# Block stages of a gated MLP: chains 256 columns wide, and weight tiles moved by 64 bytes against the activations

## The chip, the cores and the metric

The kernel runs on one core of one Trainium2 chip. Its time is the device time of one execution in microseconds (us); times of a kernel are given as the median of several runs, and one more execution is taken by the hardware profiler. A core has a matrix engine (TensorE; PE in the profile, with its weight loads shown apart as PEld), a vector engine (VectorE, DVE), a scalar engine (ScalarE, ACT), GpSimd (POOL) and SyncE (SP), which here issues most of the transfers from device memory (DMAs). They work side by side and wait for each other through semaphores. A matmul multiplies a stationary operand of 128 x 128 values, which is loaded first, with a moving operand of 128 rows and up to 512 columns, and writes or adds into a bank of PSUM. Everything else lies in SBUF, 128 partitions wide; the place of a tile is its byte address within each partition.

## The reference

Two layers over 512 rows of width 1024. Layer A mixes by a gated matrix memory and by attention to a memory of 256 rows, layer B by attention over a band of chunks and by the same kind of memory attention. Behind each mixer stands a gated MLP with a causal convolution of width 3, and this is the part that the change is about:

```python
def conv_ffn(h, w_up, conv_w, conv_b, w_down):
    u, g = jnp.split(h @ w_up, 2, axis=-1)
    g = causal_dwconv(g, conv_w, conv_b)
    return (jax.nn.silu(g) * u) @ w_down
...
        x = x + jnp.concatenate([mix_out, mem_out], axis=-1) @ w_out
        x = x + conv_ffn(rmsnorm(x, norm_ffn_g[l]), ffn_w_up[l], ffn_conv_w[l], ffn_conv_b[l], ffn_w_down[l])
```

The inner width D_FF is 2816, that is 22 tiles of 128. All data are float32.

## The kernel before

**High and low parts.** A product of float32 matrices is made of three matmuls in a faster format (fp32r): high part times high part, high times low, low times high. `split` makes the two parts: ScalarE copies the source into the high tile (line 130), VectorE subtracts it from the source into the low tile (line 131). `mm3` issues the three matmuls (lines 177, 178, 179); the order of their stationary operands is high, high, low. `load` fetches raw weights into a tile "wr" (line 143, issued by SP), and `parts` splits them into tiles "wh" and "wl", of which there are three each.

**Channel mixer.** For every tile j of the inner width the mixer computes an up and a gate product, applies the convolution and the activation, and keeps the result in `hid`. For j = 0 to 4 (`plain`) these are ordinary projections: 8 blocks of weights, 24 matmuls of 512 columns each. From j = 5 (PLAIN) to 21, 17 steps a layer, `later` and `step` use a block scheme with seven products of half size in place of eight. The rows are taken in two halves of H = 256 columns. `forms` prepares sums and differences of the activations once a layer, in "u" tiles: a tile of `self.sums` holds the high part in its first 256 columns and the low part in the others. Class `Forms` prepares the weights of a step: the upper block (`split_up`: a11, a12) and the sums (`split_sums`: s1, s3) go to wh and wl; three further forms, s2, a22 and s4, are made by `form` in two "u" tiles each.

**A step.** `step` writes out the order by hand for TensorE, ScalarE and VectorE (`manual_schedule`). Its chains on TensorE are a11, a12, s2, a down product, s1, s3, a second down product, a22, s4. Between them stand the preparation of the next step's weights (`nxt`) and the tail of the last one (`tail`: convolution, activation, gating, split). A down product is 12 matmuls of 512 columns with weights of `ffn_w_down`; steps 9 to 20 have two, steps 5 to 8 one, step 21 none. `products` is a chain over four blocks, with mm3 on 256 columns: 12 matmuls. For j in WIDE (9 to 20) the chains s2, s3 and a22 are made by `wide_products` instead: per block one matmul of the low weights with 256 columns, and one of the high weights with 512, the activations' high and low parts side by side (lines 792 and 793). The two halves of the bank are then added up: a copy by ScalarE (line 827) and an addition by VectorE (line 829).

**Places.** Tiles of one tag lie one after another in the order in which tags are first used. "u", "pt", "wr" and "t" all begin at 64 modulo 512 bytes, and so do the activations. wh and wl have rows of D + 64 values (4352 bytes, 256 more than a multiple of 512), so their three buffers begin at 64, 320 and 64 (wh) and 320, 64 and 320 (wl). `parts` takes `at=SHIFT`, 16 values or 64 bytes further, for the two splits of the block stages.

**Around the stages.** Everything outside the step loop is ordered by a planner that simulates the engines. x is kept in eight "u" tiles (`xT`), written to device memory (`xspill`), dropped, and read again by `reload_x` (line 423, on SP) behind each channel mixer and ahead of each output projection. The down products of a step are added into `xspill` by a transfer of POOL (line 761). The last six tiles of `hid` go through an ordinary projection after the loop, whose result is added to xT (line 1281 in layer A). The B layer's values are "u" tiles too (`project_pair`).

Of the kernel before, what the change touches and what calls it, by code (L numbers as in the profile page):

```python
# [9 lines left out]
F32 = mybir.dt.float32  # L10
# [6 lines left out]
P = 128  # L17
# [26 lines left out]
UNITS = {PLAIN - 1: (0, 1, 2, 3), 5: (None, 4), 6: (None, 5), 7: (None, 6), 8: (None, 7)}  # L44
UNITS.update((j, (2 * j - 10, 2 * j - 9)) for j in range(9, 21))

WIDE = range(9, 21)
H = S // 2


# [5 lines left out]
def trunk(  # L56
# [22 lines left out]
    pool = ctx.enter_context(tc.tile_pool(name="pool", bufs=1))  # L79
    psum = ctx.enter_context(tc.tile_pool(name="psum", bufs=1, space=bass.MemoryType.PSUM))  # L80

    bufs = {"wr": 3, "wh": 3, "wl": 3, "u": 57, "t": 8, "pt": 2, "s": 16, "rb": 3, "bias": 4}
    pbufs = {"mm": 3, "sc": 3, "tr": 2}
    count = [0]
    dram = ctx.enter_context(tc.tile_pool(name="dram", bufs=1, space=bass.MemoryType.DRAM))
# [1 line left out]
    def sb(tag, shape, dtype=F32):  # L87
        count[0] += 1
        return pool.tile(shape, dtype, tag=tag, name=f"{tag}{count[0]}", bufs=bufs[tag])
# [2 lines left out]
        count[0] += 1  # L92
        return psum.tile([P, S], F32, tag=tag, name=f"p{tag}{count[0]}", bufs=pbufs[tag])

    def small(n=4):
        return sb("s", [P, 32])[:, :n]


    ident = cpool.tile([P, P], F32, name="ident")
# [45 lines left out]
            nc.sync.dma_start(raw[:, :, b:], extra)  # L145
        return raw

    SHIFT = 16

    def weight_tiles(a, b, at=0):  # L150
        places = (at, at)
        return [
            sb(tag, [P, D + 64], F32R)[:, o : o + a * b].rearrange("p (a b) -> p a b", a=a)
            for tag, o in zip(("wh", "wl"), places)
        ]

    def parts(raw, pinned=False, at=0):
        _, a, b = raw.shape
        hi, lo = weight_tiles(a, b, at)
        split(hi, lo, raw, pinned=pinned)  # L160
        return hi, lo

# [68 lines left out]

    def diagonal(c):

        cs = [sb("s", [P, 32], F32R)[:, :TT] for _ in range(2)]
        split(*cs, c, on_act=False)
        dgs = []
        for c in cs:
            dg = sb("t", [P, S], F32R)
            V.tensor_tensor(
                out=dg.rearrange("p (a b) -> p a b", a=TT),  # L240
                in0=ident.unsqueeze(1).to_broadcast([P, TT, P]),
                in1=f(c).unsqueeze(2).to_broadcast([P, TT, P]),
                op=ALU.mult,
            )
            dgs.append(dg)
        return dgs
# [150 lines left out]
    def x_tile(j):  # L397
        tp = ps(("sc", "tr")[j % 2])
        for T in range(TT):
            nc.tensor.transpose(tp[:, T * P : (T + 1) * P], xr[T][:, j * P : (j + 1) * P], ident)  # L400
        xT.append(sb("u", [P, S]))
        A.copy(xT[j], tp)

    acts, scaled_x = [], []
# [14 lines left out]

    def reload_x():  # L420
        for j in range(KT):
            xT[j] = sb("u", [P, S])
            tc.keep_in_program_order(nc.sync.dma_start(xT[j], xspill[j]))

    def value_weights(hf, u):
# [222 lines left out]
    class ChannelMixer:  # L648
# [136 lines left out]

            return [(p[i - 1][:, :H], p[i - 1][:, H:]) for p in self.sums]

        def wide_products(self, r, w, i):

            n = KT // 2  # L790
            for k, p in enumerate(self.sums):
                nc.tensor.matmul(r[:, :H], w[1][:, k], p[i - 1][:, :H], start=False, stop=False, skip_group_check=True)  # L792
                nc.tensor.matmul(r, w[0][:, k], p[i - 1], start=False, stop=k == n - 1, skip_group_check=True)  # L793

        def later(self):


            prep, tail = Forms(self, PLAIN), None
            prep.sums()
            prep.split_second()  # L800
            prep.sum_third()
            prep.split_up()
            prep.split_sums()
            prep.sum_fourth()
            prep.split_down()
            prep.split_gate()
            with tc.manual_schedule(
                engines={mybir.EngineType.PE, mybir.EngineType.Activation, mybir.EngineType.DVE}
            ):
                for j in range(PLAIN, FT):  # L810
                    self.beside()
                    tail, prep = self.step(j, prep, Forms(self, j + 1) if j + 1 < FT else None, tail)
            for part in (tail.last_block, tail.first_tap, tail.second_tap, tail.third_tap, tail.gated, tail.split):
                part()

        def step(self, j, w, nxt, tail):
            def then(o, *names):
                for name in names if o is not None else ():
                    getattr(o, name)()

            def sum_products(o, r, w, i):

                if j in WIDE:
                    self.wide_products(r, w, i)
                else:
                    self.products(r, w, self.t(i))
                A.copy(o, r[:, :H])  # L827
                if j in WIDE:
                    V.tensor_tensor(out=o, in0=o, in1=r[:, H:], op=ALU.add)  # L829

            new = Tail(self, j)
            then(tail, "last_block", "first_tap")
            w.split_fourth()
            r1, r2, new.r3 = ps("mm"), ps("mm"), ps("sc")
            new.up, new.u3, new.pre = sb("t", [P, S]), sb("t", [P, S]), sb("t", [P, S])
            self.products(r1, w.a11, self.b(0, 0), True)
            A.copy(new.up[:, :H], r1[:, :H])
            then(tail, "second_tap")
            self.products(r2, w.a12, self.b(1, 0), True)
            V.tensor_tensor(out=new.up[:, :H], in0=new.up[:, :H], in1=r2[:, :H], op=ALU.add)  # L840
            then(tail, "third_tap")
            sum_products(new.up[:, H:], r1, w.s2, 2)
            then(nxt, "sums")
            then(tail, "gated")
            then(nxt, "split_second", "sum_third")
            w.down_products(0)
            self.products(new.r3, w.s1, self.t(1), True)
            w.add_down(0)
            then(tail, "split")
            then(nxt, "split_up")  # L850
            sum_products(new.u3[:, :H], r1, w.s3, 3)
            V.tensor_tensor(out=new.pre[:, H:], in0=new.u3[:, :H], in1=new.r3[:, :H], op=ALU.add)
            then(nxt, "split_sums")
            w.down_products(1)
            then(nxt, "sum_fourth")
            w.add_down(1)
            sum_products(new.pre[:, :H], r1, w.a22, 4)
            then(nxt, "split_down", "split_gate")
            self.products(new.r3, w.s4, self.b(1, 1))
            return new, nxt  # L860

    class Forms:
# [12 lines left out]
            return t[:, :n], t[:, n:]  # L875

        def form(self, src):
            hi, lo = (sb("u", [P, S], F32R).rearrange("p (a b) -> p a b", a=KT // 2) for _ in range(2))
            split(hi, lo, src)
            return hi, lo  # L880

# [13 lines left out]
            self.sub(self.halves(self.s13)[1], self.halves(self.up)[0], self.halves(self.gate)[0])  # L895

        def split_up(self):
            self.a11, self.a12 = zip(*(self.halves(t) for t in parts(self.up, at=SHIFT)))

        def split_sums(self):  # L900
            self.s1, self.s3 = zip(*(self.halves(t) for t in parts(self.s13, at=SHIFT)))

        def sum_fourth(self):
            s2, s4 = self.halves(self.s24)
# [48 lines left out]
    def channel_mixer(l, act, norm, gain, beside):  # L953

        mixer = ChannelMixer(l, act, norm, gain, beside)
        forms = mixer.forms()
        run(mixer.plain(0))
        for j in range(1, UNSCALED):
            weave(mixer.plain(j), forms, KT / (16.0 * (UNSCALED - 1)))
        until(lambda: len(mixer.ready) == KT, forms)  # L960
        mixer.buffers()
        for j in range(UNSCALED, PLAIN):
            units = UNITS.get(j, ())
            raws = {u // 2: mixer.load_down(u // 2) for u in units[::2]}
            weave(mixer.plain(j), forms, 4 / (16.0 * (PLAIN - UNSCALED)))
            for u in units:
                if u // 2 not in mixer.down:
                    mixer.down[u // 2] = parts(raws[u // 2])
                mixer.add(*mixer.down_products(u))
        run(forms)  # L970
        mixer.later()
        reload_x()
        return mixer.hid[FT - LAST :]
# [328 lines left out]
    def project_pair(j):  # L1302
        def times_row(o):
            t = sb("t", [P, S])
            V.tensor_tensor(out=t, in0=o, in1=norm.row, op=ALU.mult)
            return t

        ov = yield from project(w_kv, AW + j * P, kvact)
        t = times_row(ov) if norm.row is not None else None
        o = yield from project(w_kv, j * P, kvact)  # L1310
        if t is None:
            t = times_row(ov)
        k = head_keys(times_row(o))
        tp = ps("mm")
        for T in range(TT):
            nc.tensor.transpose(tp[:, T * P : (T + 1) * P], t[:, T * P : (T + 1) * P], ident)
        v = []
        for i in range(2):

            w = sb("u", [P, S], F32R).rearrange("p (h c) -> p h c", h=4)  # L1320
            split(w[:, :, :HD], w[:, :, HD:], tp[:, i * MEM : (i + 1) * MEM].rearrange("p (h c) -> p h c", h=4))
            v += [w[:, :2, :], w[:, 2:, :]]
        q = queries((yield from project(b_w_in, j * P, act)), norm.row)
        qkv[j] = q, k, v
# [206 lines left out]
```

## Time and profile before

| | us |
|---|---|
| three runs: median, lowest, highest | 1191.7, 1190.5, 1192.39 |
| the profiled execution | 1191.35 |
| its span, first to last instruction | 1189.6 |
| TensorE busy | 1179.0 |
| VectorE busy | 961.9 |
| ScalarE busy | 723.6 |

In rows of instruction groups, the columns are: line, engine, operation, tiles written and read (out<-in, without buffer numbers), shapes, count, then busy time in us, mean duration of one in ns, and the idle time ahead of them with what ended it. Matmuls are pipelined: the duration of one reaches from its start to the last result, and the next one starts long before that. The pace is the distance between two starts, so it is read from the timeline, whose columns are start and duration in us, engine, line, operation, tiles, count.

### The profile page before, as it was taken

To read this page: it belongs to the slowest core of one execution; us is meant where nothing else is said; L and a number is where in the kernel's file an instruction comes from. 1 tells how busy PE (TensorE), PEld (TensorE's weight loads), DVE (VectorE), ACT (ScalarE), POOL (GpSimd) and SP (SyncE) were. 2 spreads that over 40 slices of the span, in tenths; PEclk is the share of its full clock that TensorE was granted. 3 is DMA by queue.
4 is the path that set the end of the run, shared out by engine and by line. 5 is a ranking of instruction groups with operands and counts; after the bars stand their busy time and mean duration, and the time that the engine had idled before them with its cause. 6 is when DMAs were issued, how large, how long until landed. Compare 5 with 4: busy or idle time off the path is not lost.

```text
span 1189.6 us, 18184 instructions
## 1 busy us (share of the span) xinstructions
PE 1179.0 (99%) x6719; PEld 1032.1 (87%) x6719; DVE 961.9 (81%) x1760; ACT 723.6 (61%) x1294; POOL 130.0 (11%) x222
## 2 busy tenths in 40 slices
PE   9999999999999999999999999999999999999997
PEld 8988888888889988999888888888889988999986
DVE  6877688888978888888798888997896888888855
ACT  5648677655655555555576667776565655555545
POOL 1211201010021111111021000101001010111100
PEclk9999999999999999999999999999999999999999
DMA  8645313444266666666564313245326466665551
GB/s 283 212 114 133 93 55 80 146 142 135 87 160 159 158 162 158 154 145 132 145 197 131 89 53 102 70 131 184 117 89 152 107 141 142 142 141 137 123 159 71
DMA packets 200155, 158.61 MB, mean 133 GB/s; under 512 B 8344, under 2 KB 179838, under 8 KB 200066
## 3 DMA queue, kind: packets, MB, share of 16 engines
q1 hardware_dynamic: 183906, 119.74, 34.3%
q0 software_dynamic: 15584, 36.67, 15.3%
q8 instruction: 53, 0.87, 0.3%
q10 hardware_dynamic: 576, 1.05, 0.2%
q14 instruction: 36, 0.29, 0.1%
HBM read 128.89 MB, written 32.46 MB: 136 GB/s over the span
## 4 chain that ended last, share of the span: by engine, by line
PE 92%; ACT 3%; DVE 2%; DMA 2%; issue 0%; SPq 0%; POOL 0%; POOLq 0%; DVEq 0%; ACTq 0%
PE pmm L177 15%; PE pmm L178 15%; PE pmm L179 14%; PE ptr L178 6%; PE ptr L177 6%; PE ptr L179 6%; PE pmm L793 6%; PE psc L179 5%; PE psc L178 5%; PE psc L177 5%; PE pmm L792 3%; PE psc L527 2%; DMA wr<-in_mem_w_kv_dram 2%; PE ptr L1358 1%; PE ptr L1379 1%; PE ptr L1380 1%
## 5 line engine op out<-in xcount | busy, mean ns | idle before, releaser
L177 PE MATMUL pmm<-u,wh 128*128 128x512 f32 (+1 forms) x872 | 307.6, 353 | 0.3 <-ACT u L130 0.2
L179 PE MATMUL pmm<-u,wl 128*128 128x512 f32 (+1 forms) x872 | 304.7, 350 | 0.0
L178 PE MATMUL pmm<-u,wh 128*128 128x512 f32 (+1 forms) x872 | 304.6, 350 | 0.0
L131 DVE TENSOR_TENSOR wl<-wr,wh 128x1024 fp32r<-128x1024 f32 (+3 forms) x172 | 199.8, 1162 | 56.8 <-ACT wh L130 54.9
L130 ACT CAST wh<-wr 128x1024 fp32r<-128x1024 f32 (+3 forms) x172 | 171.8, 1001 | 98.4 <-PE pmm L178 44.3
L179 PEld LDWEIGHTS pmm<-u,wl 128*128 128x128 f32 x872 | 163.9, 188 | 21.0
L177 PEld LDWEIGHTS pmm<-u,wh 128*128 128x128 f32 x872 | 164.3, 189 | 18.5 <-ACT u L130 1.1
L178 PEld LDWEIGHTS pmm<-u,wh 128*128 128x128 f32 x872 | 164.2, 188 | 18.2 <-DVE u L131 0.5
L177 PE MATMUL ptr<-u,wh 128*128 128x512 f32 x272 | 106.7, 392 | 0.0
L178 PE MATMUL ptr<-u,wh 128*128 128x512 f32 x272 | 106.2, 390 | 0.0
L179 PE MATMUL ptr<-u,wl 128*128 128x512 f32 x272 | 106.0, 390 | 0.0
L761 POOL DMA_DIRECT2D xspill<-t x64 | 55.5, 867 | 454.2 <-ACT t L760 443.5
L130 ACT CAST u<-pt 128x512 fp32r<-128x512 f32 x102 | 62.7, 617 | 46.9 <-DVE pt L883 46.8
L131 DVE TENSOR_TENSOR u<-pt,u 128x512 fp32r<-128x512 f32 x102 | 69.9, 688 | 11.0 <-ACT u L130 8.3
L177 PE MATMUL psc<-u,wh 128*128 128x256 f32 (+1 forms) x232 | 75.9, 327 | 0.0
L179 PE MATMUL psc<-u,wl 128*128 128x256 f32 (+1 forms) x232 | 75.7, 326 | 0.0
L178 PE MATMUL psc<-u,wh 128*128 128x256 f32 (+1 forms) x232 | 75.6, 326 | 0.0
L793 PE MATMUL pmm<-u,u 128*128 128x512 f32 x192 | 69.9, 398 | 0.0
L945 ACT ACTIVATE t<-t 128x512 f32<-128x512 f32 x34 | 21.5, 633 | 79.4 <-DVE t L668 79.4
L829 DVE TENSOR_TENSOR t<-t,pmm 128x256 f32<-128x256 f32 x72 | 30.1, 419 | 41.8 <-ACT t L827 41.8
L760 ACT COPY t<-ptr 128x512 f32<-128x512 f32 x64 | 37.4, 585 | 42.9 <-PE ptr L179 42.8
L668 DVE SCALAR_TENSOR_TENSOR t<-t,cols,t 128x511 f32<-128x511 f32 x80 | 59.7, 746 | 3.7 <-ACT t L675 3.7
(300 smaller groups left out, 2670.6 us busy)
## 6 DMA issues: line engine op xcount, KB each, us to landing
wr<-in_ffn_w_up_dram SPq DMA_DIRECT2D x54, 512.0 KB, 4.2
wr<-in_ffn_w_down_dram SPq DMA_DIRECT2D x38, 512.0 KB, 4.1
pt<-in_ffn_w_up_dram SPq DMA_DIRECT2D x34, 512.0 KB, 6.4
xspill<-t POOLq DMA_DIRECT2D x64, 256.0 KB, 5.3
wr<-in_a_w_in_dram SPq DMA_DIRECT2D x20, 512.0 KB, 3.8
xspill<-u POOLq DMA_DIRECT2D x32, 256.0 KB, 2.7
u<-xspill SPq DMA_DIRECT2D x32, 256.0 KB, 4.8
wr<-in_w_kv_dram SPq DMA_DIRECT2D x12, 512.0 KB, 3.8
```

The lines of the kernel that those rows point to most:

```text
L130: high = A.copy(hi, src) if on_act else V.tensor_copy(hi, src)
L131: low = V.tensor_tensor(out=lo, in0=src, in1=f(hi), op=ALU.subtract)
L177: nc.tensor.matmul(o, lh, rh, start=first, stop=False, skip_group_check=more)
L178: nc.tensor.matmul(o, lh, rl, start=False, stop=False, skip_group_check=more)
L179: nc.tensor.matmul(o, ll, rh, start=False, stop=last, skip_group_check=more)
L527: nc.tensor.matmul(o, a, b, start=first and i == 0, stop=i == 1)
L668: V.scalar_tensor_tensor(acc[:, n:], src[:, : S - n], self.fw[:, c * FT + j : c * FT + j + 1], acc[:, n:], op0=ALU.mult, op1=ALU.add,)
L760: A.copy(t, o)
L761: G.dma_start(xspill[j], t, accum_op=ALU.add)
L792: nc.tensor.matmul(r[:, :H], w[1][:, k], p[i - 1][:, :H], start=False, stop=False, skip_group_check=True)
L793: nc.tensor.matmul(r, w[0][:, k], p[i - 1], start=False, stop=k == n - 1, skip_group_check=True)
L829: V.tensor_tensor(out=o, in0=o, in1=r[:, H:], op=ALU.add)
```

## The change

- `wide_products` and WIDE go; all chains of all 17 steps are made by `products`, 256 columns wide, and the additions at line 829 go with them.
- The order of tags in memory is fixed at the start by allocating one tile of each. Sizes are chosen so that the places modulo 512 come out as wanted: wh and wl become single tiles wh0, wh1, wh2 and wl0, wl1, wl2, of which the first two pairs have 16 values to spare.
- Ordinary weights take these in a ring, high and low parts both at the activations' place (64). Block weights take fixed ones, the upper block 0 and the sums 1; their high parts lie at 0, their low parts at 128 modulo 512, 64 bytes below and above the activations.
- The forms s2, a22 and s4 leave "u" for new tags "fh" (high, at 0) and "fl" (low, at 128), four buffers each. xT takes the same eight tiles, and so do the B layer's values except those of pair 5. "u" has 50 buffers in place of 57.
- Small tiles become 16 values wide instead of 32, 26 in place of 16, spread over three tags that also fill gaps between the others.
- In `later` the first step's `split_up` comes first. In the plain part the ring is moved on so that it stands right when the block stages begin.

```diff
-WIDE = range(9, 21)
...
-    bufs = {"wr": 3, "wh": 3, "wl": 3, "u": 57, "t": 8, "pt": 2, "s": 16, "rb": 3, "bias": 4}
+    HALF = 16
+    sizes = {"u": (50, S), "pt": (2, 5 * S), "wr": (3, D), "t": (8, S), "wh2": (1, D), "wl2": (1, D), "rb": (3, S)}
+    sizes.update({"bias": (4, S), "wl0": (1, D + HALF), "fl": (4, S), "s0": (6, 16), "wh0": (1, D + HALF)})
+    sizes.update({"wl1": (1, D + HALF), "s1": (6, 16), "fh": (4, S), "wh1": (1, D + HALF), "s2": (14, 16)})
+    bufs = {tag: n for tag, (n, _) in sizes.items()}
...
+    for tag, (n, size) in sizes.items():
+        pool.tile([P, size], F32, tag=tag, name=f"first_{tag}", bufs=n)
...
-    SHIFT = 16
-
-    def weight_tiles(a, b, at=0):
-        places = (at, at)
-        return [
-            sb(tag, [P, D + 64], F32R)[:, o : o + a * b].rearrange("p (a b) -> p a b", a=a)
-            for tag, o in zip(("wh", "wl"), places)
-        ]
+    turn = [0]
+
+    def weight_tiles(a, b, block=None):
+        i = turn[0] % 3 if block is None else block
+        turn[0] = i + 1
+        tiles = []
+        for tag in ("wh", "wl"):
+            t = sb(f"{tag}{i}", [P, D + HALF * (i < 2)], F32R)
+            at = HALF if i < 2 and (block is None) == (tag == "wh") else 0
+            tiles.append(t[:, at : at + a * b].rearrange("p (a b) -> p a b", a=a))
+        return tiles
...
-        xT.append(sb("u", [P, S]))
+        xT.append(sb("fh" if j < KT // 2 else "fl", [P, S]))
...
-            xT[j] = sb("u", [P, S])
+            xT[j] = sb("fh" if j < KT // 2 else "fl", [P, S])
...
-        def wide_products(self, r, w, i):
-            n = KT // 2
-            for k, p in enumerate(self.sums):
-                nc.tensor.matmul(r[:, :H], w[1][:, k], p[i - 1][:, :H], start=False, stop=False, skip_group_check=True)
-                nc.tensor.matmul(r, w[0][:, k], p[i - 1], start=False, stop=k == n - 1, skip_group_check=True)
...
+            prep.split_up()
             prep.sums()
             prep.split_second()
             prep.sum_third()
-            prep.split_up()
...
-                if j in WIDE:
-                    self.wide_products(r, w, i)
-                else:
-                    self.products(r, w, self.t(i))
+                self.products(r, w, self.t(i))
                 A.copy(o, r[:, :H])
-                if j in WIDE:
-                    V.tensor_tensor(out=o, in0=o, in1=r[:, H:], op=ALU.add)
...
-            hi, lo = (sb("u", [P, S], F32R).rearrange("p (a b) -> p a b", a=KT // 2) for _ in range(2))
+            hi, lo = (sb(tag, [P, S], F32R).rearrange("p (a b) -> p a b", a=KT // 2) for tag in ("fh", "fl"))
...
-            self.a11, self.a12 = zip(*(self.halves(t) for t in parts(self.up, at=SHIFT)))
+            self.a11, self.a12 = zip(*(self.halves(t) for t in parts(self.up, block=0)))
...
-            self.s1, self.s3 = zip(*(self.halves(t) for t in parts(self.s13, at=SHIFT)))
+            self.s1, self.s3 = zip(*(self.halves(t) for t in parts(self.s13, block=1)))
...
+        skips = -(turn[0] + 1) % 3
         for j in range(1, UNSCALED):
+            turn[0] += j <= skips
             weave(mixer.plain(j), forms, KT / (16.0 * (UNSCALED - 1)))
...
-            w = sb("u", [P, S], F32R).rearrange("p (h c) -> p h c", h=4)
+            w = sb("u" if j == 5 else ("fh", "fl")[i], [P, S], F32R).rearrange("p (h c) -> p h c", h=4)
```

More of the change, by code (lines that the diff above doesn't have):

```diff
@@ L93, in ps, with small @@
         return psum.tile([P, S], F32, tag=tag, name=f"p{tag}{count[0]}", bufs=pbufs[tag])
-    def small(n=4):
-        return sb("s", [P, 32])[:, :n]
+    for tag, (n, size) in sizes.items():
+        pool.tile([P, size], F32, tag=tag, name=f"first_{tag}", bufs=n)
+    smalls = [0]
+    def small(n=4, dtype=F32):
+        smalls[0] += 1
+        i = smalls[0] % 26
+        return sb("s0" if i < 6 else "s1" if i < 12 else "s2", [P, 16], dtype)[:, :n]
     ident = cpool.tile([P, P], F32, name="ident")
@@ L146, in load, with parts @@
         return raw
-    SHIFT = 16
-    def weight_tiles(a, b, at=0):
-        places = (at, at)
-        return [
-            sb(tag, [P, D + 64], F32R)[:, o : o + a * b].rearrange("p (a b) -> p a b", a=a)
-            for tag, o in zip(("wh", "wl"), places)
-        ]
-    def parts(raw, pinned=False, at=0):
+    turn = [0]
[8 more added lines that the diff above has]
+        return tiles
+    def parts(raw, pinned=False, block=None):
         _, a, b = raw.shape
-        hi, lo = weight_tiles(a, b, at)
+        hi, lo = weight_tiles(a, b, block)
         split(hi, lo, raw, pinned=pinned)
@@ L232, in diagonal @@
     def diagonal(c):
-        cs = [sb("s", [P, 32], F32R)[:, :TT] for _ in range(2)]
+        cs = [small(TT, F32R) for _ in range(2)]
         split(*cs, c, on_act=False)
```

## The prediction

> **What bounds the kernel now.** I read the page first: busy time by engine, then the chain that ended last.
>
> ```profile
> span 1189.6 us, 18184 instructions
> PE 1179.0 (99%) x6719; PEld 1032.1 (87%) x6719; DVE 961.9 (81%) x1760; ACT 723.6 (61%) x1294; POOL 130.0 (11%) x222
> PE 92%; ACT 3%; DVE 2%; DMA 2%; issue 0%; SPq 0%; POOL 0%; POOLq 0%; DVEq 0%; ACTq 0%
> ```
>
> TensorE is busy for 99% of the span and holds 92% of the chain that ended last. What the change is worth must therefore be read from the pace at which matmuls follow one another, and not from a wait. The mean duration of a group does not tell that pace, because matmuls overlap. I read the timeline of TensorE for two steps of the block stages: one that uses the 512-wide form (a wide step) and one that does not (a plain step). I noted where the first matmul of each chain starts, and asked for the weight loads in the stretches between these starts. Columns: stretch, its length, busy time and count of the loads, granted clock, DMA share, GB/s.
>
> ```profile
> 438.72:440.09 1.37, 1.37 (x13) 1.00 0.90 236
> 440.09:441.45 1.36, 1.36 (x13) 1.00 1.16 255
> 441.45:442.87 1.42, 1.24 (x10) 1.00 0.94 253
> 442.87:445.61 2.74, 2.25 (x13) 1.00 1.06 302
> 445.61:447.02 1.41, 1.41 (x12) 1.00 0.70 176
> 447.02:448.43 1.41, 1.23 (x9) 1.00 0.02 5
> 448.43:451.17 2.74, 2.25 (x12) 1.00 0.84 101
> 451.17:452.58 1.41, 1.22 (x8) 1.00 0.01 1
> 452.58:454.02 1.44, 1.44 (x13) 1.00 0.35 20
> ```
>
> These nine stretches are the nine chains of a wide step in the order of the code: a11, a12, s2 (wide), a down product, s1, s3 (wide), a down product, a22 (wide), s4. The counts take in neighbours that overlap a border; by the code a 256-wide chain has 12 matmuls, a wide one 4 of 256 and 4 of 512 columns, a down product 12 of 512. In the 256-wide chains loads are in progress all the time, in the others not. The plain step:
>
> ```profile
> 341.87:343.29 1.42, 1.42 (x13) 1.00 1.11 228
> 343.29:344.70 1.41, 1.41 (x13) 1.00 0.81 147
> 344.70:346.14 1.44, 1.44 (x13) 1.00 0.99 51
> 346.14:347.55 1.41, 1.41 (x13) 1.00 0.86 176
> 347.55:348.97 1.42, 1.42 (x14) 1.00 1.08 352
> 348.97:351.71 2.74, 2.25 (x13) 1.00 0.27 109
> 351.71:353.14 1.43, 1.42 (x12) 1.00 0.05 12
> 353.14:354.58 1.44, 1.44 (x13) 1.00 0.55 146
> ```
>
> Here: a11, a12, s2, s1, s3, one down product, a22, s4. Twelve matmuls of one shape at a granted clock of 1.00 take 1.36, 1.41 or 1.44 us: 113, 118 or 120 ns each. The code tells which is which. Chains whose weights lie in the "u" tiles, at the activations' own place modulo 512 bytes, take 1.43 or 1.44 (s2, a22, s4 of the plain step; s4 of the wide one). Chains in wh and wl, which SHIFT = 16 moves by 64 bytes, take 1.41 or 1.42, and in the wide step a11 and a12 take 1.36. By the tile sizes, a11 and a12 have their highs 64 and their lows 320 bytes past the activations' place in both steps, and s1 and s3 in these two steps have 320 and 64. So a shift is worth 2 ns a matmul always and 6 ns sometimes, and one place is seen at two paces. The two paces in rows, the end of a12 and the end of s4:
>
> ```profile
> 441.00 0.28 PE L179 MATMUL pmm<-u,wl 128*128 128x256 f32 x1
> 441.11 0.28 PE L177 MATMUL pmm<-u,wh 128*128 128x256 f32 x1
> 441.23 0.28 PE L178 MATMUL pmm<-u,wh 128*128 128x256 f32 x1
> 441.34 0.28 PE L179 MATMUL pmm<-u,wl 128*128 128x256 f32 x1
> ...
> 453.66 0.28 PE L177 MATMUL psc<-u,u 128*128 128x256 f32 x1
> 453.78 0.28 PE L178 MATMUL psc<-u,u 128*128 128x256 f32 x1
> 453.90 0.28 PE L179 MATMUL psc<-u,u 128*128 128x256 f32 x1
> ```
>
> Starts are 0.11 to 0.12 apart in the first group (0.34 over three) and 0.12 in the second. A floor can be read too. The down products stream 512 columns and their loads leave slack (2.25 of 2.74 busy); 2.74 / 12 is 228 ns, or 114 for 256 columns. So 113 ns is about what the stream of 256 columns needs by itself, and 118 and 120 are that plus something the weight loads add. I do not expect any place to go much below 1.36 a chain.
>
> **The change part by part.** The base is the profiled execution: 1191.35 us, 1.75 above its span and 0.35 under the median of the runs. The code has 17 steps in each of two layers: j = 9 to 20 are wide, 12 a layer, the other 5 plain. Its row confirms the count (192 and 96 matmuls at line 792, 12 in a wide step, make 24):
>
> ```profile
> L792 PE MATMUL pmm<-u,u 128*128 128x256 f32 x192 | 53.9, 281 | 0.0
> L792 PE MATMUL pmm<-u,wl 128*128 128x256 f32 x96 | 27.0, 281 | 0.0
> L829 DVE TENSOR_TENSOR t<-t,pmm 128x256 f32<-128x256 f32 x72 | 30.1, 419 | 41.8 <-ACT t L827 41.8
> ```
>
> Wide chains become 256 wide. A wide step's seven block chains add up to 1.37 + 1.36 + 1.42 + 1.41 + 1.41 + 1.41 + 1.44 = 9.82 us, a plain step's to 1.42 + 1.41 + 1.44 + 1.41 + 1.42 + 1.43 + 1.44 = 9.97. Afterwards every step has seven chains of twelve 256-wide matmuls, all with highs 64 bytes below and lows 64 above the activations' place. If c is the length of one such chain, the change is 24 x (7c - 9.82) + 10 x (7c - 9.97) = 238c - 335.4 us. It is nothing at c = 1.409, so a pace of 117.4 ns decides the sign.
>
> What c will be no row shows, for no stationary tile of these chains lies 64 bytes below its activations. The bounds are the rows nearest to it: 1.36 (highs at 64, lows at 320, its best) gives 238 x 1.36 - 335.4 = -11.7 us; 1.44 (no shift) gives +7.3. A price below 1.36 I exclude to within some hundredths by the 114 ns of the down products. Both of the new places are 64 bytes away, as in the rows at 1.36 and at 1.41. I take the lower row plus an entry cost. That 1.36 is reached by a shifted pair and held for a whole chain shows that loads can run without delaying the next matmul; what keeps other chains at 1.41 seems to be how they are entered. The wide step's a11 pays 0.01 on its way down to it. I allow 0.04 a step for entries behind other kinds of chain, two down products and the step's start: 34 x 0.04 = 1.4 us. Sum: -11.7 + 1.4 = -10.3 us.
>
> The additions behind the wide chains go: 72 of 0.419 us on VectorE. They are off the path:
>
> ```profile
> 438.72:454.02 15.30, 15.30 (x99) 13.77 (x98) 12.76 (x20) 8.71 (x17) 2.93 (x4) 1.00 0.71 158
> ```
>
> VectorE is busy 12.76 of the 15.30 us of a wide step and TensorE all of it. I price the additions at nothing. If a step shrinks to 15.0, VectorE needs 12.76 - 3 x 0.42 = 11.5 of it, so it does not become the bound.
>
> Ordinary weights move too: highs and lows, until now 256 bytes apart, both come to the activations' place. That touches the 512-wide chains, all plain projections among them. Their loads have 0.49 us of slack in 2.74; the dearest place seen adds 0.08 to twelve loads (1.44 against 1.36) and disappears in it. Zero; without that slack it would be the 0.08 a chain.
>
> Buffers: "u" goes from 57 to 50, and eight tiles "fh" and "fl" carry x, the forms and most of the B layer's values. In a step s2, a22 and s4 are three pairs on four buffers; a form of the next step takes the buffer of a chain that ended before the copy which stands ahead of its split on ScalarE, so no wait is added. The reload of x behind a layer's last step now needs the buffers of that step's forms:
>
> ```profile
> 585.81 3.81 SPq L423 DMA_DIRECT2D u<-xspill  x8
> 587.52 0.28 PE L179 MATMUL psc<-u,u 128*128 128x256 f32 x1
> 594.67 2.67 SPq L143 DMA_DIRECT2D wr<-in_ffn_w_down_dram  x2
> u<-xspill SPq DMA_DIRECT2D x32, 256.0 KB, 4.8
> L1281 DVE TENSOR_TENSOR u<-u,pmm x8: 680/686/689, 594.6 to 619.8; 128x512 f32<-128x512 f32 x8
> ```
>
> The loads are issued from 585.81 and s4 ends about 587.6. The last buffer pair is free then, its load lands at 587.6 + 4.8 = 592.4, and the eight additions that read x run from 594.6 to 619.8, one about every 3.6 us, so x is there in time. What is queued behind these loads on SP is the last two weight loads of those down products, issued at 594.67, so a hold until 587.6 is covered. Without that cover it would be up to those 2 us a layer. Splitting the upper block first, and skipping weight slots in the plain part so that the ring arrives at slot 0, can make single weight splits wait. TensorE hardly waits for splits now:
>
> ```profile
> L177 PE MATMUL pmm<-u,wh 128*128 128x512 f32 (+1 forms) x872 | 307.6, 353 | 0.3 <-ACT u L130 0.2
> ```
>
> 0.3 us of idle time in 872 matmuls. I take zero for buffers and slots together, with 3 us (2 for a reload, the rest for splits) as the dear end and -1 as the cheap one, since the order outside the block stages is newly planned.
>
> Sum: 1191.35 - 10.3 = 1181.05, and with the 0.35 to the median 1181.4; I write 1181.5.
>
> A rule speaks against the core of this. The Trainium skill, page "SBUF — State Buffer", section "Who interferes with whom", gives TensorE two independent read ports, one for the moving operand and one for weight loads, and says that it never waits on anyone. By this rule the place of a weight could not matter and the change would gain nothing, where the rows above give one shape of chain three lengths by its place. The measurement decides for the sum; what would follow if the lengths came from something else than place is the fourth rival.
>
> **The rivals.** First, a part of the chains settles at 1.36 and the rest at 1.41: a place that needs the right entry, as a11 and a12 do, which take 1.42 and 1.41 in the plain step. With half of them c is 1.385: 238 x 1.385 - 335.4 = -5.8, 1186 us. A buffer wait of 3 us on top of the forecast gives much the same.
>
> Second, all chains stay at 1.41 to 1.42, like most shifted rows: c = 1.415 gives +1.4, 1193.1 us. For it: s1, s3 and the plain step's a11 are shifted by 64 and do not get lower, and the low a11 comes right behind an unshifted s4 of a wide step, whose disturbed pace (it follows a wide chain) vanishes with the change. Against it: nothing says that 64 below behaves like 320 past.
>
> Third, the slower side: highs 64 bytes below collide like highs at the same place, so all chains take 1.44. The place is the load of the next weight beside the stream of the current matmul, the price 7 ns a matmul over the floor, and it decides from c = 1.409 on. Here the wide form, whose loads have slack (1.24 of 1.42), was the cover, and it is gone. 238 x 1.44 - 335.4 = +7.3, 1199 us. For it: 1.44 is the length of all chains in "u" that are not wide, and a place before the moving data may be read just behind or just ahead of it. Against it: every chain with 64 bytes between the two places is shorter.
>
> Fourth, the place does nothing and each chain keeps the pace that its neighbours and its position give it. Then the wide s2, s3 and a22 become 1.44, 1.41 and 1.43 as in the plain step, which costs 0.02 + 0 + 0.02 a step, 24 x 0.04 = 1.0, so 1192.7 us. Against it: in the plain step the lengths alternate with the tile that the weights lie in, and not with the neighbours.
>
> **How the numbers follow.** The forecast has 0.45 (its own range 1177 to 1186: entries and buffers from -1 to +3 with a chain between 1.345 and 1.375), the first rival 0.17, the second 0.13, the third 0.15, the fourth 0.05; 0.05 is left for waits above 3 us. What this kernel's measurement can tell from no change is 0.2%, 2.4 us. Faster by more: forecast and first rival, 0.62 less the few cases near the border, 0.60. Within: the fourth and most of the second, 0.15. Slower: the third, the rest of the second and the long waits, 0.25. The range goes from 1177 to 1196: it takes in the forecast, the first, second and fourth and the mild cases of the third; its dear end and what lies below 1.34 a chain are left out.
>
> **What would show it.** In the changed profile, cut at the chain starts, the seven block chains of a step should each take 1.35 to 1.38 us, a wide step 15.0 and a plain one 12.3. If s1 stays at 1.41 with its new place, the second rival holds; if a11 and a12 rise to 1.44, the third; if the lengths go by position and not by tile, the fourth. The 72 additions at line 829 should be gone with no change of the path, down products should stay at 2.74, and the idle time of the matmuls with block or plain weights should stay under 1 us. The prediction is wrong if the chains do not reach 1.38 or if more than 3 us of new idle time on TensorE stands between the block stages.

## The result, and the profile after

The changed kernel takes 1181.07 us (median of 4 runs, 1180.78 to 1181.44), the one before 1191.1 beside it (4 runs, 1189.84 to 1192.39). The ratio is 0.9916, with a 95% interval of 0.9899 to 0.9933: 10 us less. 1181.5 was predicted.

From the page of the changed kernel: the span, busy time by engine, the chain that ended last by engine, and a group of matmuls.

```profile
span 1179.3 us, 18676 instructions
PE 1169.1 (99%) x7007; PEld 1034.2 (88%) x7007; DVE 935.7 (79%) x1688; ACT 725.8 (62%) x1294; POOL 129.9 (11%) x222
PE 94%; DVE 3%; ACT 1%; issue 0%; DMA 0%; SPq 0%; POOL 0%; ACTq 0%; POOLq 0%; DVEq 0%
...
L194 PE MATMUL pmm<-u,wh 128*128 128x512 f32 (+1 forms) x968 | 333.2, 345 | 0.4 <-ACT u L140 0.2
```

There are 288 matmuls more (7007 against 6719; every one of 72 chains has 12 in place of 8) and 72 VectorE instructions fewer, and yet TensorE is busy for 10 us less. It is still busy for 99% of the span. So the pace has changed, not a wait. The windows of the weight loads of the changed kernel, cut at the chain starts of the same wide step as before (stretch, length, busy time and count of the loads, granted clock, DMA share, GB/s):

```profile
435.43:436.79 1.36, 1.36 (x14) 1.00 1.12 285
436.79:438.14 1.35, 1.35 (x13) 1.00 1.22 200
438.14:439.50 1.36, 1.36 (x13) 1.00 0.68 200
439.50:442.25 2.75, 2.26 (x13) 1.00 1.02 282
442.25:443.62 1.37, 1.37 (x12) 1.00 0.73 192
443.62:444.98 1.36, 1.36 (x13) 1.00 0.35 59
444.98:447.72 2.74, 2.26 (x13) 1.00 0.66 86
447.72:449.09 1.37, 1.36 (x12) 1.00 0.00 0
449.09:450.45 1.36, 1.36 (x13) 1.00 0.66 131
```

All seven block chains (a11, a12, s2, s1, s3, a22, s4) now take 1.35 to 1.37 us by these rounded borders; before, they took 1.36 to 1.44. The step is 15.02 us long in place of 15.30. The plain step that the prediction showed, likewise (a11 and s4, and the sum over all eight stretches):

```profile
340.90:342.27 1.37, 1.36 (x12) 1.00 1.10 247
...
351.82:353.19 1.37, 1.37 (x14) 1.00 0.42 123
sum 12.29, PEld 11.79; mean PEld 1.47
```

It had 12.71. The block stages as a whole, from the first to the last matmul start of each layer, with all engines; the kernel before:

```profile
341.87:587.52 245.65, 245.65 (x1626) 224.89 (x1624) 200.70 (x311) 141.00 (x243) 39.41 (x53) 1.00 0.63 147
900.64:1146.48 245.84, 245.84 (x1626) 225.03 (x1625) 201.46 (x311) 141.64 (x243) 24.70 (x29) 1.00 0.58 133
```

and the changed one:

```profile
340.91:581.54 240.63, 240.58 (x1769) 226.18 (x1768) 187.98 (x275) 142.20 (x243) 39.51 (x53) 1.00 0.67 154
895.29:1136.18 240.89, 240.84 (x1770) 226.41 (x1769) 188.78 (x275) 142.84 (x243) 24.74 (x29) 1.00 0.61 139
```

The columns behind the length are the busy time and count of PE, PEld, DVE, ACT and POOL. The two stages are 5.02 and 4.95 us shorter. The rest of the span nearly cancels: the part ahead of the first stage is 0.96 shorter (341.87 to 340.91), the part between the stages 0.63 longer (313.12 to 313.75). Together -10.3 us of span, all but 0.3 of it from the block stages.

Two small waits are new. In step 7 of each layer TensorE is held up (layer A here; timeline of the changed kernel; the value in brackets is the idle time ahead of an instruction and what ended it):

```profile
370.16 0.63 ACT L950 ACTIVATE t<-t 128x512 f32<-128x512 f32 x1 [2.53 <-DVE t L685]
370.70 0.35 ACT L834 COPY t<-pmm 128x256 f32<-128x256 f32 x1
371.11 0.19 PEld L194 LDWEIGHTS pmm<-u,wh 128*128 128x128 f32 x1 [0.24 <-ACT t L834]
371.33 0.28 PE L195 MATMUL pmm<-u,wh 128*128 128x256 f32 x1
371.45 0.28 PE L196 MATMUL pmm<-u,wl 128*128 128x256 f32 x1
```

s3 goes into the bank of s2 and waits until ScalarE has copied s2 out (line 834). That copy stands behind an activation (line 950), and this one behind a VectorE operation of the last step's tail. TensorE now arrives 0.2 us too early. Behind the hold matmuls first start 0.12 us apart (371.33 to 371.45) and not 0.113. In layer A four distances are so long, then the pace is back at 0.113 or 0.114; in layer B the slower pace (0.117 to 0.125) lasts to the end of the chain. The other wait is on VectorE: its group of additions at line 1288, which read the reloaded x, was once idle for 0.8 us until a reload into "fl" had landed. TensorE does not show that one.

### The profile page after: what moved, and what is told of

The parts are those of the page before. It is cut to its first block, busy times and chain, and to the rows that moved or that the text cites. A ratio compares the mean times of both kernels' runs of the same rounds, so it can differ in the third digit from the quotient of the medians.

```text
span 1179.3 us, 18676 instructions
## 1 busy us (share of the span) xinstructions
PE 1169.1 (99%) x7007; PEld 1034.2 (88%) x7007; DVE 935.7 (79%) x1688; ACT 725.8 (62%) x1294; POOL 129.9 (11%) x222
## 4 chain that ended last, share of the span: by engine, by line
PE 94%; DVE 3%; ACT 1%; issue 0%; DMA 0%; SPq 0%; POOL 0%; ACTq 0%; POOLq 0%; DVEq 0%
PE pmm L194 18%; PE pmm L195 18%; PE pmm L196 18%; PE ptr L195 6%; PE ptr L194 6%; PE ptr L196 6%; PE psc L195 5%; PE psc L196 5%; PE psc L194 5%; PE psc L544 2%; PE ptr L1365 1%; PE ptr L1386 1%; PE ptr L1387 1%; PE ptr L627 1%; PE ptr L613 0%; DVE pt L141 0%
## 5 line engine op out<-in xcount | busy, mean ns | idle before, releaser
L194 PE MATMUL pmm<-u,wh 128*128 128x512 f32 (+1 forms) x968 | 333.2, 345 | 0.4 <-ACT u L140 0.2
L196 PE MATMUL pmm<-u,wl 128*128 128x512 f32 (+1 forms) x968 | 330.8, 342 | 0.0
L195 PE MATMUL pmm<-u,wh 128*128 128x512 f32 (+1 forms) x968 | 330.5, 342 | 0.0
L196 PEld LDWEIGHTS pmm<-u,wl 128*128 128x128 f32 x968 | 181.9, 188 | 20.6
L194 PEld LDWEIGHTS pmm<-u,wh 128*128 128x128 f32 x968 | 181.8, 188 | 19.3 <-ACT u L140 1.1
L195 PEld LDWEIGHTS pmm<-u,wh 128*128 128x128 f32 x968 | 182.0, 188 | 18.5 <-DVE u L141 0.5
L141 DVE TENSOR_TENSOR fl<-pt,fh 128x512 fp32r<-128x512 f32 x102 | 70.3, 689 | 11.2 <-ACT fh L140 8.5
L194 PE MATMUL pmm<-u,fh 128*128 128x256 f32 x272 | 75.4, 277 | 0.0
L195 PE MATMUL pmm<-u,fh 128*128 128x256 f32 x272 | 75.2, 276 | 0.0
L196 PE MATMUL pmm<-u,fl 128*128 128x256 f32 x272 | 75.2, 276 | 0.0
L140 ACT CAST fh<-pt 128x512 fp32r<-128x512 f32 x102 | 62.7, 615 | 13.5 <-DVE pt L888 13.3
```

The costliest lines, as they stand in the source:

```text
L140: high = A.copy(hi, src) if on_act else V.tensor_copy(hi, src)
L141: low = V.tensor_tensor(out=lo, in0=src, in1=f(hi), op=ALU.subtract)
L194: nc.tensor.matmul(o, lh, rh, start=first, stop=False, skip_group_check=more)
L195: nc.tensor.matmul(o, lh, rl, start=False, stop=False, skip_group_check=more)
L196: nc.tensor.matmul(o, ll, rh, start=False, stop=last, skip_group_check=more)
```

## The experiments

The kernel before was timed again beside each group of experiments: 1190.39 us beside e1 to e4, 1190.19 beside e5 to e8, 1190.31 beside e9 to e12. Ratios are to these times; that of the change is to the 1191.1 above. All offsets are those of the block weights' high and low parts from the activations' place, in bytes; the change itself is -64 / +64. "Length" is that of a block chain that is not disturbed, from the windows cut at the chain starts. "Apart" is the distance between high and low parts. Ordinary weights lie at the activations' place in all rows. The four other experiments (e2, e6, e7, e8) differ in more than these offsets and are told in the text.

| run | highs / lows | apart | length, us | time, us | ratio to before, 95% |
|---|---|---|---|---|---|
| the change | -64 / +64 | 128 | 1.36 | 1181.07 | 0.9899 to 0.9933 |
| e5 | +64 / -64 | 128 | 1.36 | 1183.08 | 0.9916 to 0.9956 |
| e10 | +64 / +192 | 128 | 1.36 | 1183.01 | 0.9915 to 0.9960 |
| e9 | -64 / -64 | 0 | 1.41 | 1192.19 | 1.0005 to 1.0027 |
| e4 | 0 / +64 | 64 | 1.41 to 1.42 | 1192.69 | 1.0004 to 1.0031 |
| e3 | -64 / 0 | 64 | 1.41 to 1.42 | 1192.78 | 1.0002 to 1.0024 |
| e12 | -32 / +32 | 64 | 1.41 to 1.42 | 1194.78 | 1.0023 to 1.0063 |
| e1 | 0 / 0 | 0 | 1.44 | 1198.02 | 1.0038 to 1.0084 |
| e11 | -128 / +128 | 256 | 1.44 to 1.45 | 1202.85 | 1.0077 to 1.0136 |

**The narrow chains without the new places (e2).** In the kernel before:

```diff
-WIDE = range(9, 21)
+WIDE = ()
```

> The kernel before with 256-wide chains in all steps, its places unchanged. Place theory: every step looks like the old plain step, 9.97 us of chains in place of 9.82 in 24 steps, +3.6 us, about 1195 us. Rival (the wide chains disturbed the pace): all chains fall to 1.36, about 1180 us.

Measured: 1193.94 us (1193.59 to 1195.28), ratio 1.0026 [1.0015, 1.0037]. The first three stretches of the same step (a11, a12, s2):

```profile
437.92:439.33 1.41, 1.41 (x13) 1.00 1.16 232
439.33:440.74 1.41, 1.41 (x13) 1.00 1.07 223
440.74:442.18 1.44, 1.44 (x13) 1.00 0.77 171
```

The reader should see a11 and a12. They lie where they lay before, 64 and 320 past the activations, but they take 1.41, where the kernel before had 1.36. So this place has two paces, and what ran before the chain decides between them: behind the s4 of a wide step it was 1.36, behind that of a 256-wide step it is 1.41. In this order, highs and lows 256 apart at odd multiples of 64 give 1.41.

**The new layout with all block weights at the activations' place (e1).** Offsets become two constants, which pad tags and a shift inside the tile carry out; small tiles get one tag:

```diff
-    HALF = 16
+    HIGH, LOW = 0, 0
...
-        for tag in ("wh", "wl"):
-            t = sb(f"{tag}{i}", [P, D + HALF * (i < 2)], F32R)
-            at = HALF if i < 2 and (block is None) == (tag == "wh") else 0
+        for tag, d in (("wh", HIGH), ("wl", LOW)):
+            t = sb(f"{tag}{i}", [P, D + abs(d) * (i < 2)], F32R)
+            at = max(0, -d if block is None else d) if i < 2 else 0
```

> The changed kernel, all weights of the block stages at the activations' place (no 64 bytes up or down). Place theory: every 256-wide block chain takes 1.44 us, as the unshifted chains did before, so 34 x 7 x (1.44 - 1.36) = 19 us over the changed kernel, about 1200 us. Rival (the wide chains disturbed the pace, and without them any place runs at the floor): chains 1.36, about 1181 us.

Measured: 1198.02 us (1197.99 to 1198.23), ratio 1.0061 [1.0038, 1.0084].

```profile
438.59:440.03 1.44, 1.44 (x14) 1.00 1.13 230
440.03:441.47 1.44, 1.44 (x14) 1.00 1.20 213
...
442.91:445.65 2.74, 2.26 (x13) 1.00 0.98 282
```

Block chains take 1.44 and down products 2.74. The same operations in other places cost 17 us more than the change. The prediction's formula, 238c - 335.4, gives +7.3 at 1.44; against its own base the run has +7.6.

**One half of the move alone (e3, e4)**, with the constants -16, 0 and then 0, 16 (in values of 4 bytes):

> The changed kernel with high parts 64 bytes below, low parts at the activations' place. If each weight load counts for itself, 8 of 12 loads run at 113 and 4 at 120 ns: chains 1.39, about 1187 us. If the highs' place alone sets it: 1.36, 1181 us. If any low at the activations' place spoils the chain: 1.44, 1200 us.

> The changed kernel with high parts at the activations' place, low parts 64 bytes above. If each load counts for itself, 4 of 12 loads run at 113 and 8 at 120 ns: chains 1.41, about 1193 us. If the lows' place alone sets it: 1.36, 1181 us. If the highs alone count: 1.44, 1200 us.

Measured: 1192.78 us for the highs alone (ratio 1.0013 [1.0002, 1.0024]) and 1192.69 for the lows alone (1.0017 [1.0004, 1.0031]). One row of each, a12:

```profile
439.37:440.78 1.41, 1.41 (x13) 1.00 1.11 226
```

```profile
441.65:443.06 1.41, 1.41 (x13) 1.00 1.12 243
```

Against all at the same place (1198.02) each half gains some 5 us, both together 17. The halves do not add up: there are 6 us that need both. None of the three expectations for e3 fits (1.39, 1.36 or 1.44 us a chain), so the loads do not simply count one by one. The first expectation for e4, 1.41, is met, but by a rule that e3 does not follow.

**The signs swapped (e5), and both parts on one side (e6).** e5 has the constants 16, -16; e6 has -16 for both, and leaves two of the three slots of the ordinary weights 64 bytes below as well.

> The changed kernel with high parts 64 bytes above and low parts 64 below. Theory sides (highs and lows have to lie on two sides of the moving data's place): chains 1.36, about 1181 us. Theory direction (the load of the highs has to run 64 bytes behind): 1.41 or more, 1192 to 1199 us.

> The changed kernel with high and low parts both 64 bytes below (two of three ordinary weight slots lie there too). Theory sides: 1.41, about 1193 us. Theory distance (every load 64 bytes off is enough): 1.36, about 1181 us.

Measured: 1183.08 us (1182.23 to 1183.92) with the signs swapped, and 1193.19 (1192.63 to 1195.25, ratio 1.0025 [1.0014, 1.0036]) with both below. In e5 a down product, s1 and s3 read:

```profile
440.30:443.04 2.74, 2.25 (x13) 1.00 1.03 300
443.04:444.43 1.39, 1.38 (x13) 1.00 0.60 158
444.43:445.79 1.36, 1.36 (x13) 1.00 0.57 49
```

The chain right behind a down product takes 1.381 between the unrounded starts (1.39 by the borders shown), the next one 1.36: a cost of entry of 0.02, where the change pays 0.008 at that place (1.368 and 1.360). So swapped signs do nearly the same as the change (all 238 block chains take 325.8 us, 325.3 in the change), and both below do not.

**The wide chains in the new places (e7)**: `wide_products`, WIDE and the addition put back into the changed kernel.

> The changed kernel with the 512-wide form back in steps 9 to 20, at the new places. If the wide form is only dearer because its pair costs 353 ns where three 256-wide matmuls now cost 340: 288 x 13 ns = 3.7 us more, about 1185 us, other chains at 1.36. If wide chains disturb the chains behind them as they did before: some chains at 1.38 to 1.44, 1186 to 1192 us. If the wide form gains from the places too (one load in a 512-wide matmul, pair 340): 1181 us.

Measured: 1188.45 us (1186.55 to 1189.27), ratio 0.9981 [0.9968, 0.9994]. Of the wide step a11, a12, the wide s2, s1 and s4:

```profile
436.29:437.71 1.42, 1.42 (x13) 1.00 0.81 208
437.71:439.14 1.43, 1.43 (x13) 1.00 1.15 274
439.14:440.53 1.39, 1.23 (x9) 1.00 1.03 296
...
443.26:444.62 1.36, 1.36 (x12) 1.00 0.68 185
...
450.12:451.55 1.43, 1.43 (x13) 1.00 0.25 24
```

The wide chain gains by the place (1.39; between unrounded starts it took 1.413 before). But a11 and a12, at the place that gives 1.36 in the change, take 1.42 and 1.43, and so does s4 behind the wide a22. s1, behind a down product, takes 1.36. So the 256-wide chains behind a wide one (s4 and the next step's a11 and a12) run at a second, slower pace, and a down product between ends it. In step 21, which has no down product, s2, s1 and s3 take 1.43 too. The wide chains alone do not make that slow or fast, since behind them the places of before gave 1.36: it is the place and what ran before it together. The two halves of the change are worth +3.6 us (e2) and -1.7 us (e7) alone, and -10 together.

**The ordinary weights moved too (e8).** wl2 is moved behind wl0 and wh2 ahead of wh0 in the order of tags, and:

```diff
-            at = HALF if i < 2 and (block is None) == (tag == "wh") else 0
+            at = HALF if i < 2 and tag == "wl" else 0
```

> The changed kernel with the ordinary weights at the block places as well (highs 64 below, lows 64 above in all three slots). The 512-wide chains' loads have slack, so by the prediction's reading nothing changes: 1181 us. Rival: the excess of those chains over the floor (228.3 against 226.7 ns in 3002 matmuls) is the same collision, and up to 5 us go: 1176 us.

Measured: 1206.02 us (1203.88 to 1207.6), ratio 1.0133 [1.0116, 1.0150].

```profile
426.13:427.55 1.42, 1.42 (x13) 1.00 1.15 229
427.55:428.98 1.43, 1.43 (x13) 1.00 0.90 198
...
430.41:433.20 2.79, 2.25 (x13) 1.00 0.90 260
```

The down product has its slack as before (loads busy 2.25 of 2.79 us) and takes 0.05 longer. Neither expectation foresaw a loss. Counted from consecutive starts over the whole trace, 512-wide matmuls are 231.5 ns apart (228.3 in the change), 3002 x 3.2 ns = 9.6 us. The 238 block chains take 339.5 us (325.3), 14 us more; the two together are about the 22.9 us by which the span is longer. The block weights had not moved, and they can still run at the short pace: in the first step of layer B all five chains ahead of the first down product take 1.36 or 1.37. s3, that down product and a22 behind it:

```profile
914.78:916.14 1.36, 1.36 (x13) 1.00 0.97 307
916.14:918.94 2.80, 2.26 (x13) 1.00 0.05 17
918.94:920.37 1.43, 1.43 (x13) 1.00 0.00 0
```

From there on every block chain of the layer takes 1.42 or more. In the change a down product leads back to the short pace; with its weights moved it leads to the slow one. The block chains lose more by it (14 us) than the 512-wide matmuls themselves (9.6).

**What the place has to be (e9 to e12).** Four more pairs of constants: -16, -16 with the ordinary weights at the activations' place; 16, 48; -32, 32; -8, 8. "u" has one buffer fewer (49).

> As the run with both parts 64 bytes below, but with every ordinary weight back at the activations' place, and one u buffer fewer. Theory sides (highs and lows must lie on different sides of the moving data, or 128 bytes apart): block matmuls at 118 ns, about 1193 us. Rival (the moved ordinary weights had spoilt that run): 113 ns, about 1181 us.

> The changed kernel with highs 64 and lows 192 bytes above, so 128 apart on one side, and one u buffer fewer. Theory sides: 118 ns, about 1193 us. Theory 128 apart: 113 ns, about 1181 us.

> The changed kernel with highs 128 bytes below and lows 128 above, and one u buffer fewer. Theory sides: 113 ns, about 1181 us. Theory 128 apart (they are 256 apart here): 118 to 120 ns, 1193 to 1199 us.

> The changed kernel with highs 32 bytes below and lows 32 above, and one u buffer fewer. Theory sides: 113 ns, about 1181 us. If the distance has to be 64: between 113 and 120 ns, 1181 to 1199 us, and the nearer to 120 the coarser the steps in which places count.

Measured: 1192.19, 1183.01, 1202.85 and 1194.78 us; e11 is slower than both of its expectations. Of e10 a11, then the down product and the two chains behind it:

```profile
436.40:437.76 1.36, 1.36 (x13) 1.00 0.91 210
...
440.49:443.23 2.74, 2.25 (x13) 1.00 1.03 300
443.23:444.61 1.38, 1.38 (x12) 1.00 0.67 173
444.61:445.97 1.36, 1.36 (x13) 1.00 0.55 43
```

Of e11 and e12 a11 and the first down product:

```profile
440.15:441.59 1.44, 1.44 (x14) 1.00 1.08 223
...
444.47:447.23 2.76, 2.25 (x13) 1.00 1.00 290
```

```profile
437.91:439.32 1.41, 1.41 (x13) 1.00 1.18 241
...
442.15:444.93 2.78, 2.26 (x13) 1.00 0.90 260
```

e9 leaves out e6's move of ordinary weights and keeps its length, 1.41. e10 has both parts above the activations and reaches 1.36, so the two need not lie on different sides. e11 lies on both sides, 256 apart, and is as slow as no shift at all. In e11 and e12 the down products, whose weights lie where the change has them, take 2.76 and 2.78.

So the chains settled at the short length in the three cases in which high and low parts are 128 bytes apart and each an odd multiple of 64 from the activations, and in none of the six others, nor in e2 (256 apart; there the ordinary weights' parts lie 256 apart too, so its surroundings differ). In these runs a pair 256 apart does as a pair 0 apart: 1.41 in e2 and e9, 1.44 or a little more in e11 and e1. Whether 128 apart is enough by itself is not settled: 128 apart with one part at the activations' own place, or at offsets that are no multiples of 64, was not tried.

But no place is tied to one length. +64 / +320 had 1.36 in the kernel before and 1.41 in e2. In step 21 a22 has to wait for ScalarE's copy of s3, in the kernel before, in the change and in e6 alike, and the next chain, s4, can leave its usual pace then: at -64 / -64 it takes 1.36 (e6, layer B), and at the change's own place 1.43 (layer A), as the chains of e7 and e8 do. The two rows, e6 first:

```profile
1146.43:1147.79 1.36, 1.36 (x13) 1.00 0.45 87
```

```profile
580.23:581.66 1.43, 1.43 (x13) 1.00 0.60 171
```

What the table shows is therefore the pace into which this order of chains settles at a place, and not what a place allows. Why the distance between two stationary tiles and the entry matter at all stays open.

## Why the prediction held, and which of its reasons did not

**The bound and the formula: right.** TensorE's pace decides. Counted from all starts, the 238 block chains took 335.4 us before (as the prediction had it from two steps) and 325.3 after, so -10.1 us; the 56 down products added 0.15. At the other end e1 bears the formula out (+7.3 by it, +7.6 measured), at the middle e3 and e4: c = 1.415 gives +1.4, and +2.4 and +2.3 were measured.

**The chain's length c: the right number, with luck.** The prediction took 1.36 because a11 and a12 had it in a wide step, at a shifted place, and held that "what keeps other chains at 1.41 seems to be how they are entered". That much is borne out: with the same place and another entry, e2 has 1.41. What had no ground was the next step, that in the new order the chains at the new place would be entered the good way, but for 0.04 a step. In e2 the new order leads every shifted chain into the slow pace, and at -64 / +64 it could have led to 1.43, as in e7 and e8. That it settles at 1.36 is due to the new pair of offsets (other pairs in the same order settle at 1.41 or 1.44) together with the place of the ordinary weights (e8). Nothing in the trace of before could tell this, for every shifted pair in it is 256 apart. The second rival was right that the low a11 came from the disturbed s4 of a wide step, but its conclusion, all at 1.41, held for the old places alone.

**The entry cost: right in size (+1.4 us predicted), wrong in kind.** In the changed kernel 230 of the 238 chains take 1.360 us, or 1.368 behind a down product: entry costs 0.4 us in all. The other eight take 1.43 to 1.57: s1 and s3 of step 7, and a22 and s4 of step 21, in each layer. They hold 12.06 - 8 x 1.362 = 1.2 us. 0.7 of it is the hold in step 7 and the slower pace behind it, the rest the same in step 21. That one isn't new: a22 of step 21 took 1.54 and 1.52 before (1.52 in both layers now). So the 1.4 was met by the sum of a small entry cost and two holds that it did not mean. In e5 and e10 the entry behind a down product costs 0.02.

**The additions at nothing: right.** VectorE has 188 us of work in a stage of 240.6 (200.7 of 245.65 before).

**The ordinary weights' move at nothing: the number held, the reason failed.** The prediction said that the slack of 512-wide chains would swallow the dearest place. e8 moves just these weights and costs 25 us against the change (1206.02 and 1181.07), with that slack in plain sight. In the change they come to lie at the activations' place, highs and lows together, and there down products stay at 2.74 to 2.75. An idle load queue doesn't show that the stream is undisturbed.

**Buffers and the reload: nearly right.** The bounds were -1 and +3 us; the only new hold found on TensorE is that of step 7, 0.7 us in both layers together, and no other block chain but those of step 21 takes above 1.37 us. The matmuls that a late split holds up stood for 0.4 us in 968 (0.3 in 872 before; the row at line 194 above). The reload went as described, in the SyncE queue of the changed kernel:

```profile
580.31 1.76 SPq L440 DMA_DIRECT2D fh<-xspill  x2
582.13 2.92 SPq L440 DMA_DIRECT2D fl<-xspill  x4
588.70 3.67 SPq L153 DMA_DIRECT2D wr<-in_ffn_w_down_dram  x2
```

The last loads are issued behind the last form's chain (s4 runs from 580.23 to 581.66). The weight loads behind them are issued 8.5 us behind the start of s4, as before (588.70 and 594.67, where s4 started at 586.20), so they are not held up.

**The rivals.** The first, a place that needs the right entry, names what the runs show, but in the change's order only the chains behind holds miss the short pace. The third, all at 1.44, was priced at 1199 us; e1, where all chains do take 1.44, is at 1198.02. Its length is there, but at the activations' own place and not 64 below it; that weight loads collide with the stream, as this rival has it, no run shows. The fourth, that the place does nothing, falls with e1 against the change. But the neighbours that it names do set the pace as well: in e7 and e8 chains in the change's own place take 1.42 and 1.43.

**The rule that was weighed.** The Trainium skill, page "SBUF — State Buffer", section "Who interferes with whom", says that TensorE reads moving data and weights through two independent ports and never waits on anyone. The measurement decides against its use here: equal instructions take 1198.02 or 1181.07 us by the place of the weights alone.

## What to carry to other kernels

Where TensorE is busy all the time, read the distance between starts, by tile and by place, before looking for waits: here the same matmul was 113, 118 or 120 ns from the next. A shift is to be tried on the pair, highs and lows together, and beside the neighbours that it will have, since halves of a good change (e2, e3, e4, e7) were each worth little or were losses. A pace that one group of chains reaches in a mixed order is no proof of its place; the place has to be run in the order in which it will be used.

## What the runs showed of the hardware that was not expected

- The pace of 256-wide matmuls depends on where high and low stationary tiles lie relative to each other, not only relative to the moving data. With each an odd multiple of 64 bytes from the moving data, the chains settle at 1.36 us at 128 apart and at 1.41 at 0 (e9, both at -64) and 256 (e2).
- The pace has a memory. The same place holds 1.36 or 1.43 (the change, e7), 1.36 or 1.41 (before and e2), for whole chains. After the hold in step 7 of layer B matmuls stay about 0.118 us apart where the undisturbed chain has 0.113, and after the wide a22 in e7 the next three chains take 1.42 to 1.43. A down product ended it there; with its weights moved (e8) a down product brought it about.
- The same offsets that make 256-wide chains shortest make 512-wide ones longer: 228.3 to 231.5 ns a matmul in e8.
- No block chain of any run took less than 1.36 us.
